# Seven products of quarters in place of a full product in the gated unit of a two-layer trunk

## Chip, core and metric

The kernel runs on one core of a Trainium2 chip. The metric is device time in microseconds (us) of one execution, given as the median of repeated runs. TensorE (PE) multiplies into PSUM; VectorE (DVE), ScalarE (ACT) and GpSimd (POOL) do the elementwise work; all transfers are issued from the queue of SyncE (SP).

## Reference

The reference is a two-layer encoder trunk over 1024 tokens of width 1024, float32. What matters here is the end of the first branch of layer 0 (a state-space layer) and its neighbours:

```
y = gelu(y)                                            # (1024, 1024)
y = y * sigmoid(y @ glu_w + glu_b)                     # the gated unit
y_s5 = y * silu(g_s5)
y_ret = retention(q, k, v) * silu(g_ret)
x = x + concatenate([y_s5, y_ret], -1) @ w_out
```

Layer 1 (a convolution module) and a last RMSNorm follow.

## The kernel before

Activations are kept transposed: channels in 8 blocks of 128 partitions, tokens in two halves of 512 columns. Every large product is made in three matmuls of 128x128 weights by 512 columns (`mm3`, L161 to L168): weights and activations are each split into a high part, rounded on ACT, and a low part, the difference, made on DVE or POOL; high x high, high x low and low x high are added up in one PSUM bank. Products go to three banks (`ps_mm`) in turn.

*Weights* come from one list in program order (`plan`, L75). `wnext` (L105) asks for a weight and issues loads up to two ahead. `wload_pieces` (L146) loads 512 KB into one of three `wf` buffers, rounds it on ACT into one of three `wh` (L157), and makes the low part into one of three `wl` (L158), on POOL except for the names in `LO_V` (L34), which go to DVE. A `wf` buffer is free once both have read it.

*Layer 0* first runs the input projections and the state-space layer (`layer0_front`), which leave y, the gates and the retention's inputs in DRAM. Then `retention` (L860) goes over four pairs of heads: `ret_proj` (L896) projects k and q, multiplies them by the row scale on DVE (L909), swaps halves of the heads by four small DMAs (L918), and turns them on POOL (L922, L924) and DVE (L925). For pair 0 `ret_values_wide` (L961) makes values for two pairs from eight weights, each used for 24 matmuls; pairs 2 and 3 have their own two weights (`ret_values`, L942). Per pair, `y_pass` (L851) takes two blocks of y through the GELU on ACT (L857) into `yn_d` in DRAM. `ret_heads` (L983) does the scores, the state, the norm and the gate, and stores `yr_d`.

*The gated unit* stands at the head of `layer0_back_and_layer1` (L1097). `load_split` (L1107) loads 16 tiles of `yn_d` (8 blocks by 2 halves), two to a `wf` buffer, and splits them (L1092 to L1095) into the operand tiles `opA`. For each of the 8 output blocks, one weight serves two products of 24 matmuls, one for each half (L1135 to L1151): tanh on ACT from PSUM (L1146); gate times y on POOL (L1142) from two loads, `yg` (2 buffers, L1139) and `yn` (3 buffers, L1141); product on DVE (L1147) in one of five `sg` buffers; and the split into `ys` on ACT and DVE (L1149, L1150). Then `yr_d` is loaded and split (L1152), and `w_out` (L1158) multiplies `ys` and `yr` by the output weights.

The order of instructions on each engine is set by a planner that simulates the program with the program's order as priority. `issue_after` forces an instruction behind another one; a DRAM tile that is read waits for its writer. On every engine and in the SP queue the order that results is kept at run time.

Of the kernel before, what the change touches and what calls it, by code (L numbers as in the profile page):

```python
# [19 lines left out]
P = 128  # L20
D = 1024
T = 1024
# [29 lines left out]
class Trunk:  # L52
# [22 lines left out]
    def plan(self):  # L75
# [11 lines left out]
        seq += [(A["w_glu"][nb], f"glu{nb}") for nb in range(8)]  # L87
# [98 lines left out]
    def run(self):  # L186
# [27 lines left out]
        self.yr_d = dt("yr_d", [D, T])  # L214
        self.x1_d = dt("x1_d", [D, T])
# [635 lines left out]
    def y_pass(self, rp, cb):  # L851

        nc = self.nc
        yt = rp.tile([P, 8, P], F32, name=f"yp_{cb}", tag="yp", bufs=1)
        nc.sync.dma_start(yt[:], self.y_d[cb].rearrange("i h g m -> (h g) i m"))
        yn = rp.tile([P, P, 8], F32, name=f"yn_{cb}", tag="ynt", bufs=1)
        nc.scalar.activation(yn[:], yt[:].rearrange("p i m -> p m i"), AF.Gelu_apprx_tanh)  # L857
        nc.sync.dma_start(self.yn_d[cb * P:(cb + 1) * P], yn[:].rearrange("p m i -> p (m i)"))

    def retention(self, st):  # L860
# [13 lines left out]
        for pair in range(4):  # L874
# [21 lines left out]
    def ret_proj(self, pair):  # L896
        nc, A, rp = self.nc, self.A, self.rp
        tq = self.rq.tile([P, 2, T], F32, name=f"ropeq_{pair}", tag="ropeq", bufs=1)
# [3 lines left out]
        def project(nm):  # L902
            w = self.wnext(f"{nm}{pair}")
            raw = raws[nm] = self.rq.tile([P, T], F32, name=f"{nm}raw_{pair}", tag="raw", bufs=2)
            for h in range(2):
# [3 lines left out]
                last = nc.vector.tensor_tensor(raw[:, c], ps[:], self.R[:, c], op=ALU.mult)  # L909
            return last  # L910

        def turn(nm, behind=None):
# [3 lines left out]
            for b in range(4):  # L916
                s = b ^ 1
                nc.sync.dma_start(swp[32 * b:32 * b + 32, :], raw[32 * s:32 * s + 32, :])  # L918
# [4 lines left out]
            for c in cs:  # L923
                nc.gpsimd.tensor_tensor(swp[:, c], swp[:, c], tab[:, 1, c], op=ALU.mult)  # L924
# [15 lines left out]
        yield krot, qrot, qadds  # L940
# [20 lines left out]
    def ret_values_wide(self):  # L961
# [622 lines left out]
```

## Time and profile before

| | |
|---|---|
| median of 3 runs | 1204.49 us (1203.98 to 1204.63) |
| profiled execution | 1205.3 us, of which 1203.5 us from the first to the last instruction |
| mean granted TensorE clock | 0.999 |
| first and last matmul of the gated unit start at | 549.7 and 649.6 us |
| DMA, whole span | 234.19 MB, 195 GB/s mean |

Busy time is the time in which an engine has an instruction in work; for matmuls, which are pipelined, it overlaps. A row of the profile names line, engine, operation, output and inputs, shape, and either one instruction's start and length or a group's count, total and mean. "Idle before" names what ended an engine's wait.

### The profile page before, as it was taken

To read this page: it belongs to the slowest core of one execution; us is meant where nothing else is said; L and a number is where in the kernel's file an instruction comes from. 1 tells how busy PE (TensorE), PEld (TensorE's weight loads), DVE (VectorE), ACT (ScalarE), POOL (GpSimd) and SP (SyncE) were. 2 spreads that over 40 slices of the span, in tenths; PEclk is the share of its full clock that TensorE was granted. 3 is DMA by queue.
4 is the path that set the end of the run, shared out by engine and by line. 5 is a ranking of instruction groups with operands and counts; after the bars stand their busy time and mean duration, and the time that the engine had idled before them with its cause. 6 is when DMAs were issued, how large, how long until landed. Compare 5 with 4: busy or idle time off the path is not lost.

```text
span 1203.5 us, 17285 instructions
## 1 busy us (share of the span) xinstructions
PE 1191.8 (99%) x6442; PEld 999.4 (83%) x6442; DVE 799.5 (66%) x1389; ACT 477.5 (40%) x699; POOL 637.9 (53%) x441
## 2 busy tenths in 40 slices
PE   9999999999999999999999999999999999999997
PEld 7888888888888889998888888888888888888877
DVE  7975798777411457447546322599999799899533
ACT  7212223222223233143435322545535675434652
POOL 2059999988146254242441110678453567758642
PEclk9999999999999999999999999999999999999999
DMA  9344355565385175477448875766678664357774
GB/s 336 105 127 146 102 168 177 184 177 171 108 286 177 53 214 164 148 210 258 157 140 272 302 266 201 245 210 208 211 246 279 204 191 154 114 183 237 238 265 146
DMA packets 105364, 234.19 MB, mean 195 GB/s; under 512 B 9536, under 2 KB 40000, under 8 KB 104640
## 3 DMA queue, kind: packets, MB, share of 16 engines
q1 hardware_dynamic: 105280, 233.09, 58.5%
q8 instruction: 50, 0.82, 0.3%
q14 instruction: 34, 0.28, 0.1%
HBM read 166.80 MB, written 62.06 MB: 190 GB/s over the span
## 4 chain that ended last, share of the span: by engine, by line
PE 95%; DMA 2%; DVE 1%; ACT 1%; issue 0%; POOL 0%; SPq 0%; DVEq 0%; POOLq 0%; ACTq 0%
PE mm_g L166 7%; PE mm_g L167 7%; PE mm_g L168 7%; PE mm_wo L168 5%; PE mm_wo L166 5%; PE mm_wo L167 5%; PE mm_b L167 2%; PE mm_b L168 2%; PE mm_a L167 2%; PE mm_a L168 2%; PE mm_b L166 2%; PE mm_a L166 2%; PE mm_u L168 2%; PE mm_u L167 2%; PE mm_u L166 2%; PE mm_glu L166 2%
## 5 line engine op out<-in xcount | busy, mean ns | idle before, releaser
L1270 DVE SCALAR_TENSOR_TENSOR cv<-u,convw,cv 128x512 f32<-128x512 f32 x398 | 273.4, 751 | 11.9 <-ACT cv L1256 9.6
L1250 POOL TENSOR_TENSOR tp<-tp,tp 128x512 f32<-128x512 f32 x64 | 83.0, 1297 | 44.1 <-ACT tp L1249 43.0
L166 PE MATMUL mm_g<-xh,wh_g 128*128 128x512 f32 x256 | 101.8, 398 | 0.0
L168 PE MATMUL mm_g<-xh,wl_g 128*128 128x512 f32 x256 | 100.1, 391 | 0.0
L167 PE MATMUL mm_g<-xl,wh_g 128*128 128x512 f32 x256 | 100.0, 391 | 0.0
L1249 ACT ACTIVATE tp<-u,convw 128x512 f32<-128x512 f32 x64 | 45.7, 720 | 36.1 <-POOL tp L1250 34.5
L393 POOL TENSOR_TENSOR s1q<-s1q,s1q 128x512 f32<-128x512 f32 x12 | 17.5, 1455 | 78.2 <-ACT s1q L388 78.2
L166 PEld LDWEIGHTS mm_g<-xh,wh_g 128*128 128x128 f32 x256 | 48.0, 188 | 11.7 <-issue 1.2
L168 PEld LDWEIGHTS mm_g<-xh,wl_g 128*128 128x128 f32 x256 | 48.1, 188 | 10.4
L167 PEld LDWEIGHTS mm_g<-xl,wh_g 128*128 128x128 f32 x256 | 48.1, 188 | 9.9 <-issue 0.4
L168 PE MATMUL mm_oc<-zh,wl_woc 128*128 128x512 f32 (+1 forms) x152 | 54.2, 359 | 1.0 <-DMA wl_woc<-lo_woc 1.0
L167 PE MATMUL mm_oc<-zl,wh_woc 128*128 128x512 f32 (+1 forms) x152 | 54.4, 360 | 0.5 <-POOL zl L1095 0.5
L166 PE MATMUL mm_oc<-zh,wh_woc 128*128 128x512 f32 (+1 forms) x152 | 54.1, 361 | 0.0
L1142 POOL TENSOR_TENSOR yg<-yg,yn 128x512 f32<-128x512 f32 x16 | 22.6, 1412 | 57.2 <-DMA yg<-gs_d 28.2
L167 PE MATMUL mm_u<-xl,wh_u 128*128 128x512 f32 x128 | 50.1, 391 | 1.0 <-DVE xl L281 1.0
L349 DVE TENSOR_TENSOR gt<-mm_g,R 128x512 f32<-128x512 f32 x32 | 21.9, 683 | 43.6 <-PE mm_g L168 43.6
L166 PE MATMUL mm_g<-h1h,wh_cg 128*128 128x512 f32 x128 | 50.4, 394 | 0.0
L166 PE MATMUL mm_glu<-yh,wh_glu 128*128 128x512 f32 x128 | 50.3, 393 | 0.0
L166 PE MATMUL mm_b<-h1h,wh_cb 128*128 128x512 f32 x128 | 50.2, 392 | 0.0
L166 PE MATMUL mm_wo<-yrh,wh_wor 128*128 128x512 f32 x128 | 50.2, 392 | 0.0
L168 PE MATMUL mm_a<-h1h,wl_ca 128*128 128x512 f32 x128 | 50.2, 392 | 0.0
L168 PE MATMUL mm_wo<-yrh,wl_wor 128*128 128x512 f32 x128 | 49.9, 390 | 0.0
(417 smaller groups left out, 3613.8 us busy)
## 6 DMA issues: line engine op xcount, KB each, us to landing
wf_g<-w_ab SPq DMA_DIRECT2D x16, 512.0 KB
wf_wos<-w_out SPq DMA_DIRECT2D x16, 512.0 KB
wf_wor<-w_out SPq DMA_DIRECT2D x16, 512.0 KB
wf_cb<-w_c SPq DMA_DIRECT2D x16, 512.0 KB
wf_ca<-w_c SPq DMA_DIRECT2D x16, 512.0 KB
wf_woc<-w_out_c SPq DMA_DIRECT2D x16, 512.0 KB
wf_v<-w_v SPq DMA_DIRECT2D x12, 512.0 KB
wf_cg<-w_c SPq DMA_DIRECT2D x11, 512.0 KB
```

The source lines that it names most:

```text
L166: nc.tensor.matmul(ps, wh[:, kb, :], xh, start=start, stop=False)
L167: nc.tensor.matmul(ps, wh[:, kb, :], xl, start=False, stop=False)
L168: self.last_mm = nc.tensor.matmul(ps, wl[:, kb, :], xh, start=False, stop=stop)
L349: nc.vector.tensor_tensor(gt[:, c], ps[:], self.R[:, c], op=ALU.mult)
L393: nc.gpsimd.tensor_tensor(a, a, sq[:], op=ALU.add)
L1142: gp.tensor_tensor(yg[:], yg[:], yn[:], op=ALU.mult)
L1249: nc.scalar.mul(sk[:], u[:, k:k + HALF], cw[:, nb, k:k + 1])
L1250: gp.tensor_tensor(s0[:], s0[:], sk[:], op=ALU.add)
L1270: v.scalar_tensor_tensor(dst[:], *tap, accs_[i][:], op0=ALU.mult, op1=ALU.add)
```

## The change

The product y @ glu_w is made by Strassen's scheme. With the weights in quarters (by input and output channels) and y in quarters (by channels and token halves), seven products of sums of quarters take the place of eight products of quarters. Each product is four blocks of 12 matmuls.

- `glu_sums`, called four times during retention (after the projections of pairs 0, 2 and 3, and between the two halves of the wide values), loads a quarter of the weights' data in two transfers of 512 KB into two `wf` tiles, makes the four sums in place on DVE behind the pair's last projected q, and stores them to `ws_d` in DRAM behind the last swap.
- `y_pass` takes blocks k and k + 4 in pair k, makes four sums of y in place on POOL behind the last turn, and stores them to `t_d`.
- Masks and decays of retention are loaded per pair instead of once.
- In the gated unit, 28 tiles (seven operands of four) are loaded and split in place of 16, and 14 weights, each used for 24 matmuls, are asked for in place of 8, each used for 48. Four products are copied to `u2` on ACT; sums of products are built in `u2` and `u3` on DVE; the tanh now reads from SBUF a sum that DVE makes from a bank and `u2` or `u3` (`gated`).
- In `w_out` the first block's order is the plain one.

```diff
-        seq += [(A["w_glu"][nb], f"glu{nb}") for nb in range(8)]
+        self.ws_d = self.dram.tile([2, 2, P, 2, KB, P], F32, name="ws_d")
+        quad = lambda i, j, m: A["w_glu"][i, m, :, j]
+        sums = lambda n, m: self.ws_d[n // 2, m, :, n % 2]
+        glu = [q for m in range(2) for q in (quad(0, 0, m), quad(0, 1, m))]
+        glu += [q(m) for q in (lambda m: sums(0, m), lambda m: sums(2, m), lambda m: quad(1, 1, m)) for m in range(2)]
+        glu += [sums(n, m) for m in range(2) for n in (3, 1)]
+        seq += [(q, f"glu{i}") for i, q in enumerate(glu)]
...
-    def y_pass(self, rp, cb):
-
-        nc = self.nc
-        yt = rp.tile([P, 8, P], F32, name=f"yp_{cb}", tag="yp", bufs=1)
-        nc.sync.dma_start(yt[:], self.y_d[cb].rearrange("i h g m -> (h g) i m"))
-        yn = rp.tile([P, P, 8], F32, name=f"yn_{cb}", tag="ynt", bufs=1)
-        nc.scalar.activation(yn[:], yt[:].rearrange("p i m -> p m i"), AF.Gelu_apprx_tanh)
-        nc.sync.dma_start(self.yn_d[cb * P:(cb + 1) * P], yn[:].rearrange("p m i -> p (m i)"))
+    def y_pass(self, rp, k):
+
+
+        nc, gp = self.nc, self.nc.gpsimd
+        yns = []
+        for i, cb in enumerate((k, k + 4)):
+            yt = rp.tile([P, 8, P], F32, name=f"yp_{cb}", tag="yp", bufs=1)
+            nc.sync.dma_start(yt[:], self.y_d[cb].rearrange("i h g m -> (h g) i m"))
+            yn = rp.tile([P, P, 8], F32, name=f"yn_{cb}", tag="ynt", bufs=2)
+            nc.scalar.activation(yn[:], yt[:].rearrange("p i m -> p m i"), AF.Gelu_apprx_tanh)
+            yn = yn[:].rearrange("p m i -> p (m i)")
+            nc.sync.dma_start(self.yn_d[cb * P:(cb + 1) * P], yn)
+            yns.append(yn)
+        (b11, b12), (b21, b22) = ((y[:, :HALF], y[:, HALF:]) for y in yns)
+        with self.tc.issue_after(self.last_turn.ins):
+            gp.tensor_tensor(b22, b22, b12, op=ALU.subtract)
+            gp.tensor_tensor(b12, b12, b11, op=ALU.subtract)
+            gp.tensor_tensor(b11, b22, b11, op=ALU.add)
+            gp.tensor_tensor(b21, b11, b21, op=ALU.subtract)
+        for i in range(2):
+            nc.sync.dma_start(self.t_d[i, k * P:(k + 1) * P], yns[i])
+
+    def glu_sums(self, g):
+
+        nc, v = self.nc, self.nc.vector
+        m, c = g // 2, slice(g % 2 * 4, g % 2 * 4 + 4)
+        q = [self.wp.tile([P, 2, HALF], F32, name=f"wf_gs{i}_{g}", tag="wf", bufs=3) for i in range(2)]
+        for i in range(2):
+            nc.sync.dma_start(q[i][:], self.A["w_glu"][i, m, :, :, c].rearrange("p j k n -> p j (k n)"))
+        (a11, a12), (a21, a22) = ((t[:, 0, :], t[:, 1, :]) for t in q)
+
+        with self.tc.issue_after(self.last_raw.ins):
+            v.tensor_tensor(a22, a21, a22, op=ALU.add)
+            v.tensor_tensor(a21, a11, a21, op=ALU.subtract)
+            v.tensor_tensor(a11, a22, a11, op=ALU.subtract)
+            v.tensor_tensor(a12, a12, a11, op=ALU.subtract)
+        with self.tc.issue_after(self.last_swap.ins):
+            for i in range(2):
+                nc.sync.dma_start(self.ws_d[i, m, :, :, c].rearrange("p j k n -> p j (k n)"), q[i][:])
...
-        self.mask = rp.tile([P, NH, P], F32, name="retmask")
-        nc.sync.dma_start(self.mask[:], A["ret_mask"])
-        self.kdec = rp.tile([P, NH, 64], F32, name="kdec")
-        nc.sync.dma_start(self.kdec[:], A["ret_kdec"])
...
+            if pair != 1:
+                self.glu_sums(pair)
             if pair == 0:
                 V = self.ret_values_wide()
...
-                for cb in (2 * pair, 2 * pair + 1):
-                    self.y_pass(rq, cb)
+                self.y_pass(rq, pair)
...
+        mask = rp.tile([P, 2, P], F32, name=f"retmask_{pair}", tag="retmask", bufs=2)
+        nc.sync.dma_start(mask[:], A["ret_mask"][:, 2 * pair:2 * pair + 2])
+        kdec = rp.tile([P, 2, 64], F32, name=f"kdec_{pair}", tag="kdec", bufs=2)
+        nc.sync.dma_start(kdec[:], A["ret_kdec"][:, 2 * pair:2 * pair + 2])
...
+            if h:
+                self.glu_sums(1)
...
-        def load_split(src, name, halves):
-            res = [[], []]
-
-            def put(kb, h, f):
-                a, b = (self.op_tile(self.opA, f"A{h}", f"{name}{q}{kb}_{h}") for q in "hl")
-                self.split(f, a, b, v, None if halves or h == 0 else self.last_kt if kb < 6 else self.masked[0])
-                res[h].append((a, b))
-            for h in range(2):
-                for kb in range(KB):
-                    if halves:
-                        f = lp.tile([P, HALF], F32, name=f"{name}f{kb}_{h}", tag="tp", bufs=3)[:]
-                        nc.sync.dma_start(f, src[rows(kb), hs(h)])
-                    else:
-
-                        if kb % 2 == 0:
-                            f2 = self.wp.tile([P, 2, HALF], F32, name=f"{name}f{kb}_{h}", tag="wf", bufs=3)
-                        f = f2[:, kb % 2, :]
-                        nc.sync.dma_start(f, src[rows(kb), hs(h)])
-                    put(kb, h, f)
+        def load_split(parts, name, h, wide, behind=None):
+
+            res = []
+            for i, part in enumerate(parts):
+                if wide:
+                    if i % 2 == 0:
+                        f2 = self.wp.tile([P, 2, HALF], F32, name=f"{name}f{i}", tag="wf", bufs=3)
+                    f = f2[:, i % 2, :]
+                else:
+                    f = lp.tile([P, HALF], F32, name=f"{name}f{i}", tag="tp", bufs=3)[:]
+                nc.sync.dma_start(f, part)
+                a, b = (self.op_tile(self.opA, f"A{h}", f"{name}{q}{i}") for q in "hl")
+                self.split(f, a, b, v, behind)
+                res.append((a, b))
...
-        ys_in = load_split(self.yn_d, "y", False)
+
+        B = lambda j, h: [self.yn_d[rows(4 * j + k), hs(h)] for k in range(4)]
+        S = lambda i, h: [self.t_d[i, rows(k), hs(h)] for k in range(4)]
+        b11, b21 = load_split(B(0, 0), "y11", 0, True), load_split(B(1, 0), "y21", 0, True)
         ys = [[None] * KB for _ in range(2)]
-        ws = {}
-
-        for nb, h in [(nb, h) for nb in range(6) for h in range(2)] + [(6, 0), (7, 0), (6, 1), (7, 1)]:
-            if h == 0:
-                ws[nb] = self.wnext(f"glu{nb}")
+
+        u2 = [lp.tile([P, HALF], F32, name=f"gu2_{n}", tag=tag, bufs=1) for n, tag in enumerate(("cq", "cs", "pilot", "sq"))]
+        u3 = [opB.tile([P, HALF], F32, name=f"gu3_{n}", tag="B1") for n in range(4)]
+        nw = iter(range(14))
+        wn = lambda: self.wnext(f"glu{next(nw)}")
+
+        def product(ps, w, a, x):
+            for k in range(4):
+                self.mm3(ps[:], w, 4 * a + k, (x[k][0][:], x[k][1][:]), k == 0, k == 3)
+
+        def gated(nb, h, z):
             yg = lp.tile([P, HALF], F32, name=f"yg{nb}_{h}", tag="ld", bufs=2)
             nc.sync.dma_start(yg[:], self.gs_d[rows(nb), hs(h)])
             yn = lp.tile([P, HALF], F32, name=f"yn{nb}_{h}", tag="ev", bufs=3)
             nc.sync.dma_start(yn[:], self.yn_d[rows(nb), hs(h)])
             gp.tensor_tensor(yg[:], yg[:], yn[:], op=ALU.mult)
-            ps = self.bank(f"mm_glu{nb}_{h}", aux=False)
-            self.gemm(ps[:], ws[nb], ys_in[h])
             sg = lp.tile([P, HALF], F32, name=f"sg{nb}_{h}", tag="u", bufs=5)
-            nc.scalar.activation(sg[:], ps[:], AF.Tanh, scale=0.5, bias=hgb[:, nb:nb + 1])
+            ps, other, op = z
+            v.tensor_tensor(sg[:], other[:], ps[:], op=op)
+            nc.scalar.activation(sg[:], sg[:], AF.Tanh, scale=0.5, bias=hgb[:, nb:nb + 1])
             v.scalar_tensor_tensor(sg[:], sg[:], 1.0, yg[:], op0=ALU.add, op1=ALU.mult)
             a, b = (self.op_tile(opB, f"B{h}", f"ys{q}{nb}_{h}") for q in "hl")
             nc.scalar.mul(a[:], sg[:], 0.5)
-            glu_end = v.scalar_tensor_tensor(b[:], sg[:], 0.5, a[:].bitcast(F32), op0=ALU.mult, op1=ALU.subtract)
             ys[h][nb] = (a, b)
-        yr = load_split(self.yr_d, "yr", True)
+            return v.scalar_tensor_tensor(b[:], sg[:], 0.5, a[:].bitcast(F32), op0=ALU.mult, op1=ALU.subtract)
+
+        for m in range(2):
+            for i, x in ((1, b11), (2, b21)):
+                w = wn()
+                if m == 0 and i == 1:
+                    t2 = load_split(S(0, 0), "yt2", 1, True, self.last_kt)
+                elif i == 1:
+                    t3 = load_split(S(1, 1), "yt3", 1, True, self.masked[0])
+                for a in range(2):
+                    n = 2 * m + a
+                    ps = self.bank(f"mm_glu{i}{n}", aux=False)
+                    product(ps, w, a, x)
+                    if i == 1:
+                        nc.scalar.copy(u2[n][:], ps[:])
+                    else:
+                        gated(n, 0, (ps, u2[n], ALU.add))
+        t4 = load_split(S(1, 0), "yt4", 0, False)
+        for i, x in ((6, t2), (7, t3), (4, t4)):
+            for m in range(2):
+                w = wn()
+                for a in range(2):
+                    n = 2 * m + a
+                    ps = self.bank(f"mm_glu{i}{n}", aux=False)
+                    product(ps, w, a, x)
+                    if i == 4:
+                        gated(4 + n, 0, (ps, u3[n], ALU.subtract))
+                    else:
+                        v.tensor_tensor((u2 if i == 6 else u3)[n][:], u2[n][:], ps[:], op=ALU.add)
+            if i == 6:
+                t1, b22 = load_split(S(0, 1), "yt1", 0, False), load_split(B(1, 1), "y22", 1, False)
+        for m in range(2):
+            for i, x in ((5, t1), (3, b22)):
+                w = wn()
+                for a in range(2):
+                    n = 2 * m + a
+                    ps = self.bank(f"mm_glu{i}{n}", aux=False)
+                    product(ps, w, a, x)
+                    if i == 5:
+                        gated(4 + n, 1, (ps, u3[n], ALU.add))
+                        v.tensor_tensor(u2[n][:], u2[n][:], ps[:], op=ALU.add)
+                    else:
+                        glu_end = gated(n, 1, (ps, u2[n], ALU.add))
+        yr = [load_split([self.yr_d[rows(k), hs(h)] for k in range(KB)], f"yr{h}", h, False) for h in range(2)]
...
-                if nb == 0:
-                    seq.append(seq.pop(KB - 1))
...
-    A["w_glu"] = _blocks(inp["s5_glu_w"][0][s5p][:, s5p])
+
+    wg = inp["s5_glu_w"][0][s5p][:, s5p].reshape(2, 4, P, 2, 2, 2, P)
+    A["w_glu"] = np.ascontiguousarray(wg.transpose(3, 4, 2, 0, 5, 1, 6)).reshape(2, 2, P, 2, KB, P)
```

More of the change, by code (lines that the diff above doesn't have):

```diff
@@ L214, in run @@
         self.yr_d = dt("yr_d", [D, T])
+        self.t_d = dt("t_d", [2, HALF, T])
         self.x1_d = dt("x1_d", [D, T])
@@ L908, in project @@
                 self.gemm(ps[:], w, self.xs[h])
-                last = nc.vector.tensor_tensor(raw[:, c], ps[:], self.R[:, c], op=ALU.mult)
-            return last
+                self.last_raw = nc.vector.tensor_tensor(raw[:, c], ps[:], self.R[:, c], op=ALU.mult)
+            return self.last_raw
         def turn(nm, behind=None):
@@ L939, in ret_proj @@
             qadds = ()
-        yield krot, qrot, qadds
+        yield krot, qrot, qadds, mask, kdec
     def ret_values(self, pair):
@@ L981, in ret_values_wide, with ret_heads @@
         return lambda p, b, hh: res[b // 4][:, b % 4, (2 * p + hh) * P:(2 * p + hh + 1) * P]
-    def ret_heads(self, pair, K, Q, qadds, V, turned):
+    def ret_heads(self, pair, K, Q, qadds, mask, kdec, V, turned):
         nc, rp = self.nc, self.rp
@@ L992, in ret_heads @@
                 nc.tensor.transpose(ps[:, b * P:(b + 1) * P], K[:, t0:t0 + P], self.ident[:])
-            kd = self.kdec[:, 2 * pair:2 * pair + 2, :].rearrange("p h d -> p (h d)")
+            kd = kdec[:].rearrange("p h d -> p (h d)")
             self.last_kt = v.tensor_tensor(kt[:, 4 * hf:4 * hf + 4, :], ps[:].rearrange("p (b d) -> p b d", b=4),
@@ L1035, in ret_heads @@
                     sc[hh][:, 4 * hf:4 * hf + 4, :], sps[hh][:].rearrange("p (b i) -> p b i", b=4),
-                    self.mask[:, 2 * pair + hh, :].unsqueeze(1).broadcast_to([P, 4, P]), op=ALU.mult)
+                    mask[:, hh, :].unsqueeze(1).broadcast_to([P, 4, P]), op=ALU.mult)
         gts = []
```

4 lines of the change are left out of this document (2 added, 2 removed).

## Prediction

> **What bounds the kernel now.** I read the profile page first: span and engine shares, then the chain that ended last.
>
> ```profile
> span 1203.5 us, 17285 instructions
> ...
> PE 1191.8 (99%) x6442; PEld 999.4 (83%) x6442; DVE 799.5 (66%) x1389; ACT 477.5 (40%) x699; POOL 637.9 (53%) x441
> ...
> PE 95%; DMA 2%; DVE 1%; ACT 1%; issue 0%; POOL 0%; SPq 0%; DVEq 0%; POOLq 0%; ACTq 0%
> ```
>
> TensorE (PE) idles 1203.5 - 1191.8 = 11.7 us in the whole span, and the chain of waits is 95% PE. So removed PE work is worth its full length as long as nothing new starves PE, and each new PE stall costs its full length too. Busy time of overlapping matmuls says nothing of their price, so I took the pace from the starts in the timeline of PE, inside the gated unit:
>
> ```profile
> 593.37 0.39 PE L166 MATMUL mm_glu<-yh,wh_glu 128*128 128x512 f32 x1
> 593.60 0.39 PE L167 MATMUL mm_glu<-yl,wh_glu 128*128 128x512 f32 x1
> 593.82 0.39 PE L168 MATMUL mm_glu<-yh,wl_glu 128*128 128x512 f32 x1
> 594.05 0.39 PE L166 MATMUL mm_glu<-yh,wh_glu 128*128 128x512 f32 x1
> ```
>
> Three matmuls in 0.68 us: 0.2267 us each. Next, the busy time of the engines by stage (columns: length, then busy us and count of PE, PEld, DVE, ACT, POOL, then clock, DMA share, GB/s):
>
> ```profile
> 333.00:365.00 32.00, 32.00 (x154) 26.53 (x151) 6.28 (x7) 9.40 (x8) 14.97 (x11) 1.00 0.82 263
> 365.00:400.00 35.00, 35.00 (x159) 28.99 (x158) 4.70 (x3) 11.79 (x16) 18.72 (x8) 1.00 0.52 175
> 581.20:603.00 21.80, 21.80 (x98) 18.00 (x97) 12.46 (x12) 8.11 (x12) 10.46 (x6) 1.00 0.53 181
> ```
>
> The first two rows are retention's first projections and wide values, where the first weight sums are put; the third is the gated unit behind the last heads. Other engines have room, but DMA is at 0.82 in the first. The clock is full, so no price needs scaling. Last, the timelines of ACT, POOL and the DMA queue, for the two places where new work meets old:
>
> ```profile
> 364.11 1.03 ACT L157 CAST wh_v<-wf_v 128x1024 fp32r<-128x1024 f32 x1
> ...
> 360.80 2.85 POOL L158 TENSOR_TENSOR wl_v<-wf_v,wh_v 128x1024 fp32r<-128x1024 f32 x1
> ...
> 365.13 0.98 SPq L155 DMA_DIRECT2D wf_v<-w_v  x1
> ...
> 554.86 6.68 DMA wf_glu<-w_glu
> ...
> 586.24 2.40 POOL L158 TENSOR_TENSOR wl_glu<-wf_glu,wh_glu 128x1024 fp32r<-128x1024 f32 x1
> 586.29 2.90 DVE L1147 SCALAR_TENSOR_TENSOR sg<-sg,yg 128x512 f32<-128x512 f32 x1 [4.17 <-POOL yg L1142]
> ...
> 598.60 0.32 SPq L1139 DMA_DIRECT2D yg<-gs_d  x1
> ```
>
> A weight is loaded only when a subtraction has freed one of three `wf` buffers (360.80 + 2.85 = 363.65, load at 365.13). And a VectorE (DVE) instruction with two SBUF inputs that starts beside a POOL one ends 0.6 us after it (586.29 + 2.90, against 586.24 + 2.40), though it takes 0.68 us alone.
>
> **The change, part by part.**
>
> *Products.* Before: 8 blocks x 2 halves x 8 x 3 = 384 matmuls. After: 7 products x 4 blocks x 4 x 3 = 336. 48 x 0.2267 = **-10.9 us**, all on the chain. The diff leaves no doubt that 336 are issued.
>
> *Weight sums* (`glu_sums`, four calls): each loads 2 x 512 KB into two of the three `wf` buffers, runs 4 additions on DVE behind the last projected `q`, and stores 2 x 512 KB behind the swaps. 16 additions at 0.68 us (alone) to 1.76 (the median of the rotary additions, L925, beside POOL) are 11 to 28 us of DVE, in a stage where DVE is busy 6.28 of 32 and 4.70 of 35 us: covered. What is not covered is the buffers. For pair 0 the calls stand in the program ahead of the third weight of the values, so the buffers freed at about 318 and 333 go to the sums, the third weight (`v002`) gets that of 349 and the fourth (`v003`) that of 363.65, loaded at 365.13 as now a later one is. PE wants `v003` three weights of 24 matmuls after 355.66, at 355.66 + 3 x 5.44 = 372.0. It would be ready at 365.13 + landing + 1.05 (ACT) + 2.40 to 2.85 (POOL). Landing is 3 us (a 256 KB gate load issued at 598.60 is used by POOL at 601.53) to 6.68 us (the chain's row): 371.6 to 375.7, a stall of 0 to 3.7 us. I take **1.5**, as DMA is busy there. The next weights use buffers that the stores give back from about 367 on, 5.44 us apart. The second call, between the value halves, takes the buffers of `v003` and `v010` at about 374 and 377; loads, additions and stores (3 + 3 + 4 us) give them back by about 388, and the last values weight, loaded then, is ready at 388 + 3 + 1.05 + 2.4 = 394.5, wanted at 355.66 + 7 x 5.44 + 1.5 = 395.2: nothing, at most 3 us if the load takes 6.68. The calls of pairs 2 and 3 find weights prefetched over 20 us ahead (`k3` is cast at 469.64 and used from about 494): nothing. If this cover is gone, see the slower rival. The stores wait in SP's queue for DVE; behind them stand the weight loads, which are in the same sum.
>
> *Sums of y*: 16 POOL additions at 1.29 us (L924) = 20.6 us, 5.2 per pair, behind both GELUs of the pair and the last rotary product. POOL is busy 14.97 of 32 and 18.72 of 35 us in the stages above, so they fit; 8 stores of 512 KB stand on SP behind them. The pair's weights, queued behind on POOL, have 5 us of lead: nothing. *Mask and decay by pair*: 8 loads in place of 2, same bytes; six more issues of 0.7 us on SP (L868), used tens of us later: nothing.
>
> *Operands*: 28 splits of y in place of 16: 12 x (0.62 us ACT + 0.69 DVE). 14 weights in place of 8: 6 x (512 KB, 1.05 us ACT, 2.4 to 2.6 us POOL). A weight now lasts PE 5.44 us instead of 10.88; its three `wh` buffers leave 10.9 us for a chain of 1.05 + 2.4 us: 7 us of slack. *Combinations*: 16 additions ahead of the tanh and 12 accumulations on DVE from PSUM at 0.69 us = 19 us, and 4 copies on ACT. A bank must be read within two further products, 5.4 us. *Order of w_out's first block*: `ys` of half 0 is complete after product 4, 22 us earlier: nothing.
>
> *The last twelve products* (4, then 5 and 3 in turn) are all gated: 12 x 2.72 = 32.6 us of PE. POOL: 12 gate products at 1.29 + 4 weights at 2.40 = 25.1 us. DVE with two SBUF inputs: 24 at 0.69 + 2 output weights at 1.22 + 4 splits at 0.69 = 21.7 us. If these two never overlap, 46.8 us must pass in 32.6, so the gated chain ends 14.2 us late. Five `sg` buffers let it lag five products (13.6 us), the banks only two (5.4 us). The stall lies between 0 (lag taken up by `sg`) and 14.2 - 5.4 = 8.8 us. The nearest row, 581.20:603.00, has POOL and DVE at 22.9 us together in 21.80 with PE never idle, so I keep to the lower half: **3 us**. The gate tiles have two buffers: a load is used 2.9 us after issue, then 1.29 + 0.69 us, with waits some 5.5 to 6.5 us per buffer, 2.7 to 3.3 per product against 2.72: within the same lag, not counted again. DMA in these 32.6 us: 24 x 256 KB + 5 x 512 KB + some 2 MB = 11 MB, 330 GB/s; the busiest slice of the page shows 336, so it holds with little over.
>
> [...]
>
> **Sum.** The profiled execution is 1205.3 us, its span 1203.5 and 1.8 around it, 0.8 above the median 1204.49. 1205.3 - 10.9 + 1.5 + 3 = 1198.9; less 0.8: **1198.1**, told as 1198. Bounds: 1204.5 - 10.9 = 1193.6, with all stalls nil, to 1193.6 + 3.7 + 3 + 8.8 = 1209.1.
>
> **Rivals.**
> *All hidden*: no new stall, 1193.6. For it: lags above are bounded by buffers that may suffice; against: DMA at 0.82 where the first sums load.
> *Port-bound tail*: PE waits for banks 8.8 us in the last twelve products; 1193.6 + 8.8 + 1.5 = 1203.9, within the noise. For it: the stretched DVE rows. Against: before, lags of that kind never reached PE.
> *Weights starved in the wide values (slower)*: with two of three `wf` buffers held from load to store, each values weight goes through one buffer: 6.68 + 1.05 + 2.4 = 10.1 us against 5.44 of PE, 4.7 us short each; four such weights are 19 us, 1193.6 + 19 = 1212.6, and with the tail's 3 us 1216. It decides from more than two starved weights (10.9 us). For it: one queue, 0.82 of DMA, stores waiting on DVE. Against: DVE is idle from 365 to 400, so a buffer is held some 12 us, not longer, and two calls, not four, fall in this stage.
>
> **How the numbers follow.** About 0.2% (2.4 us) is what can be told from no change: faster means below 1202.1, slower above 1206.9. Chances: forecast with stalls of 1 to 8 us 0.50; all hidden 0.20; port-bound tail or a like sum 0.10; starved weights 0.20. Faster 0.70, same 0.10, slower 0.20. The range goes from 1193, just under all hidden, to 1210, over the upper bounds and the start of the starved case.
>
> **What would show it.** Right: 336 `mm_glu` matmuls; the value weights' wait near 372 a few us at most; PE's waits inside the last products on banks read by DVE, some us in total; DVE rows of L1147's and L1150's kind with means above 1 us. Wrong: PE idle over 10 us in the wide values (starved); a gap at the first output product, on `wor` or the late splits of `yr`, which I cost at nothing; or PE time in the gated unit not lower by 10.9 us.

## The result, and the profile after

The changed kernel takes 1225.88 us (median of 6 runs, 1221.15 to 1227.66) against 1204.17 us before (1203.59 to 1204.63): ratio 1.0169, 95% interval 1.0156 to 1.0183 (the quotient of the two medians is 1.0180). The forecast was 1198.0, so the result lies 27.9 us above it and 15.9 us above the range. The profiled execution took 1222.3 us, its span 1220.5, so what is explained here are the 17.0 us between the two spans. The median stands 3.6 us higher still: four of the six executions took 1225.2 to 1227.7 us, with a mean granted clock of 0.989 to 0.994 against 0.995 in the profiled one, and what makes them longer is not shown.

Head of the page, and head of the chain, after:

```profile
span 1220.5 us, 17411 instructions
...
PE 1189.3 (97%) x6394; PEld 993.2 (81%) x6394; DVE 849.8 (70%) x1445; ACT 494.6 (41%) x723; POOL 678.9 (56%) x463
...
PE 85%; DVE 6%; DMA 5%; issue 2%; ACT 2%; SPq 0%; POOL 0%; DVEq 0%; ACTq 0%
```

48 matmuls are gone (x6442 to x6394), but idle time of PE rose from 11.7 to 1220.5 - 1189.3 = 31.2 us, and the chain has 15% that is not PE where it had 5%. Where, is told by the windows (columns as before the change):

```profile
365.00:400.00 35.00, 33.66 (x147) 27.06 (x146) 6.23 (x6) 11.05 (x13) 23.62 (x13) 1.00 0.80 273
581.20:603.00 21.80, 17.99 (x79) 14.13 (x78) 19.00 (x44) 11.57 (x17) 7.75 (x4) 0.92 0.40 126
609.00:621.00 12.00, 8.38 (x37) 6.64 (x37) 12.00 (x12) 6.12 (x11) 7.74 (x4) 1.00 0.77 273
```

In the wide values PE idles 1.3 of 35 us. In the gated unit it idles 3.8 of 21.8 us and 3.6 of 12, and there VectorE, which I had at 12.46 of 21.80, is busy 19.00 of 21.80 and then all 12.00. Note 0.92 in the clock's column. The waits of PE (what it waited for, total us, times, longest) name VectorE nearly alone. `S` are the retention's states:

```profile
PE mm_glu L172 <- DVE gu L1224: 4.6, 2, 3.6
PE mm_glu L172 <- DVE sg L1190: 4.0, 3, 2.3
PE sp L1069 <- DVE S L1062: 2.9, 1, 2.9
PE mm_glu L172 <- DVE gu L1236: 2.3, 2, 1.6
PE mm_wo L172 <- DVE gu L1236: 1.8, 1, 1.8
...
PE mm_v L1016 <- ACT wh_v L163: 1.3, 1, 1.3
```

To put a size on each stage I take the starts of PE's groups. The first product starts at 552.22 (before 549.73): 2.5 us lost ahead of it, 2.1 of them in the wide values (45.59 against 43.53). From there to the last of the heads' transposes, PE needs 0.2267 us per product matmul and 13.0 us for the heads (before: 100.1 - 384 x 0.2267); what is above is "lost in heads". This stretch holds the first two products as well: of its waits in the changed kernel (0.9, 2.9, 0.9 and 2.3 us), the last, at 586.43, is a product's wait for a bank. From there to the first output product only matmuls stand; what is above 0.2267 each is "lost in products". After: 10.2 and 14.4 us. So -10.9 + 2.5 + 10.2 + 14.4 + 0.8 (behind the unit) = +17.0.

How a product waits shows in the timeline around the longest wait:

```profile
616.27 2.80 POOL L164 TENSOR_TENSOR wl_glu<-wf_glu,wh_glu 128x1024 fp32r<-128x1024 f32 x1
...
616.78 2.83 DVE L1196 SCALAR_TENSOR_TENSOR ysl<-sg,ysh 128x512 fp32r<-128x512 f32 x1
...
619.54 0.68 DVE L1136 TENSOR_TENSOR y22l<-y22f,y22h 128x512 fp32r<-128x512 f32 x1
620.14 1.27 DVE L1224 TENSOR_TENSOR gu<-gu,mm_glu 128x512 f32<-128x512 f32 x2
...
620.96 0.47 PE L172 MATMUL mm_glu<-yt3h,wh_glu 128*128 128x512 f32 x1 [3.62 <-DVE gu L1224]
...
622.02 0.63 PE L172 MATMUL mm_glu<-yt3h,wh_glu 128*128 128x512 f32 x1
622.44 0.63 PE L173 MATMUL mm_glu<-yt3l,wh_glu 128*128 128x512 f32 x1
```

`ysl` has two SBUF inputs, begins beside a POOL subtraction and ends 0.54 us after it, 2.83 us instead of 0.68. Behind it in order stands a split, and only then the sums (`gu`) that free two banks. PE, with all three banks full, waits 3.62 us. When it resumes, its starts lie 0.43 us apart in place of 0.227, until about 624.6: eight such steps cost 1.6 us more, and the granted clock falls to 0.50.

The heads lose in the same manner:

```profile
560.63 2.53 POOL L164 TENSOR_TENSOR wl_glu<-wf_glu,wh_glu 128x1024 fp32r<-128x1024 f32 x1 [0.86 <-ACT wh_glu L163]
...
561.30 4.22 DVE L1136 TENSOR_TENSOR yt2l<-yt2f,yt2h 128x512 fp32r<-128x512 f32 x4 [0.38 <-ACT yt2h L1134]
...
562.68 0.62 ACT L1134 CAST yt2h<-yt2f 128x512 fp32r<-128x512 f32 x1 [0.26 <-DMA yt2f<-t_d]
563.65 0.62 ACT L1134 CAST yt2h<-yt2f 128x512 fp32r<-128x512 f32 x1 [0.35 <-DMA yt2f<-t_d]
...
565.45 0.28 DVE L1060 COPY S<-kv 128x128 f32<-128x128 f32 x1
...
567.02 1.23 PE L1069 MATMUL sp<-qrot,krot 64*128 64x128 f32 x8 [2.93 <-DVE S L1062]
```

Four splits of `yt2`, an operand first needed 30 us later (at 597.25), stand ahead of the states `S` that the scores wait for. The first of them has two SBUF inputs beside a POOL subtraction, takes 2.42 us and ends 0.56 us after it; the other three follow at 0.60 us each. The casts wait 0.26 and 0.35 us for their loads, but the last is done at 564.27, before its split begins at 564.84.

### The profile page after: what moved, and what is told of

It reads as the page before. It is cut to its first block, busy times and chain, and to the rows that moved or that the text cites. A ratio compares the mean times of both kernels' runs of the same rounds, so it can differ in the third digit from the quotient of the medians.

```text
span 1220.5 us, 17411 instructions
## 1 busy us (share of the span) xinstructions
PE 1189.3 (97%) x6394; PEld 993.2 (81%) x6394; DVE 849.8 (70%) x1445; ACT 494.6 (41%) x723; POOL 678.9 (56%) x463
## 4 chain that ended last, share of the span: by engine, by line
PE 85%; DVE 6%; DMA 5%; issue 2%; ACT 2%; SPq 0%; POOL 0%; DVEq 0%; ACTq 0%
PE mm_g L172 7%; PE mm_g L174 7%; PE mm_g L173 7%; PE mm_wo L172 5%; PE mm_wo L173 5%; PE mm_wo L174 5%; PE mm_b L172 2%; PE mm_b L173 2%; PE mm_a L174 2%; PE mm_b L174 2%; PE mm_a L172 2%; PE mm_a L173 2%; PE mm_u L174 2%; PE mm_u L173 2%; PE mm_u L172 2%; PE mm_oc L174 2%
## 5 line engine op out<-in xcount | busy, mean ns | idle before, releaser
L174 PE MATMUL mm_g<-xh,wl_g 128*128 128x512 f32 x256 | 100.1, 391 | 0.0
L164 POOL TENSOR_TENSOR wl_glu<-wf_glu,wh_glu 128x1024 fp32r<-128x1024 f32 x14 | 36.7, 2622 | 39.3 <-ACT wh_glu L163 36.4
L172 PEld LDWEIGHTS mm_g<-xh,wh_g 128*128 128x128 f32 x256 | 48.0, 188 | 11.7 <-issue 1.2
L172 PE MATMUL mm_wo<-ysh,wh_wos 128*128 128x512 f32 x128 | 50.0, 391 | 1.8 <-DVE gu L1236 1.8
L164 POOL TENSOR_TENSOR wl_v<-wf_v,wh_v 128x1024 fp32r<-128x1024 f32 x12 | 28.9, 2406 | 40.4 <-ACT wh_v L163 40.4
L173 PE MATMUL mm_b<-h1l,wh_cb 128*128 128x512 f32 x128 | 50.3, 393 | 0.0
L172 PE MATMUL mm_a<-h1h,wh_ca 128*128 128x512 f32 x128 | 50.2, 392 | 0.0
```

The costliest lines, as they stand in the source:

```text
L164: lo[i].tensor_tensor(wl[:].rearrange(fl)[:, c], wf[:, c], h.bitcast(F32), op=ALU.subtract)
L172: nc.tensor.matmul(ps, wh[:, kb, :], xh, start=start, stop=False)
L173: nc.tensor.matmul(ps, wh[:, kb, :], xl, start=False, stop=False)
L174: self.last_mm = nc.tensor.matmul(ps, wl[:, kb, :], xh, start=False, stop=stop)
```

## The experiments

Ratios are against the kernel before on the same chip (its median there: 1204.4 to 1205.0 us, and 1204.2 for the change). Most intervals reach 1 to 3 us to either side, so a difference between two of these kernels is good to about 3 us: 10 or 12 us are clear, 1 or 2 us are not. The losses, in us, are from one profiled execution each, worked out as above. That execution lies near the median for most, but 3.6 us below it for the change, 3.1 below for e12, 4.3 above for e2 and 5.9 above for e4.

| kernel | median | ratio, 95% interval | first product | lost in heads | lost in products |
|---|---|---|---|---|---|
| after | 1225.9 | 1.0169 [1.0156, 1.0183] | 552.2 | 10.2 | 14.4 |
| e1 products alone | 1216.3 | 1.0100 [1.0082, 1.0118] | 549.3 | 5.6 | 14.0 |
| e2 preparation alone | 1214.7 | 1.0094 [1.0074, 1.0115] | 556.6 | 6.0 | 0.1 |
| e3 sum in PSUM | 1214.0 | 1.0076 [1.0054, 1.0098] | 553.2 | 11.5 | 2.8 |
| e4 fourth call early | 1227.6 | 1.0201 [1.0168, 1.0234] | 560.4 | | |
| e5 = e1 + e3 | 1204.0 | 0.9995 [0.9985, 1.0004] | 549.3 | 6.4 | 2.6 |
| e11 e3 without sums of y | 1208.8 | 1.0042 [1.0023, 1.0062] | 551.8 | 8.7 | 2.2 |
| e12 e3 without sums of weights | 1207.9 | 1.0029 [1.0017, 1.0041] | 551.1 | 5.9 | 2.6 |
| e13 e5, two operands less | 1197.6 | 0.9938 [0.9923, 0.9953] | 549.5 | -0.5 | 1.6 |
| e14 e3, two operands less | 1203.9 | 0.9995 [0.9983, 1.0006] | 552.8 | 2.3 | 2.0 |
| e16 e3, operands regrouped | 1208.7 | 1.0040 [1.0026, 1.0055] | 553.6 | 4.2 | 5.1 |

**Products or preparation (e1, e2).** e1 takes out the sums; e2 keeps them and puts the gated unit of before back, with its 16 tiles of y, 8 weights and 384 matmuls.

In e1:

```diff
-        sums = lambda n, m: self.ws_d[n // 2, m, :, n % 2]
+        sums = lambda n, m: quad(n // 2, n % 2, m)
...
-            gp.tensor_tensor(b22, b22, b12, op=ALU.subtract)
...
-            if pair != 1:
-                self.glu_sums(pair)
...
-        S = lambda i, h: [self.t_d[i, rows(k), hs(h)] for k in range(4)]
+        S = lambda i, h: [self.yn_d[rows(4 * i + k), hs(h)] for k in range(4)]
```

In e2:

```diff
-        seq += [(q, f"glu{i}") for i, q in enumerate(glu)]
+        seq += [(A["w_glu0"][nb], f"glu{nb}") for nb in range(8)]
...
```

> The sums are left out (no weight sums, no sums of y, none of their loads and stores; the seven products take plain quarters), the gated unit keeps its 336 matmuls, 14 weights, 28 splits and all VectorE work. Theory P (the preparation holds the weight buffers and makes the operands late): the 24 us lost in the gated unit are mostly gone, 1194 to 1200 us. Theory V (VectorE, shared with POOL, is too slow for the unit's own work: bank reads, splits and gating in one queue): the loss stays, 1212 to 1222 us.

> All sums of weights and of y are made and stored as in the changed kernel, but the gated unit is the old one with 384 matmuls, 8 weights, 16 splits, and does not read them. Theory P: most of the loss shows here too, 1212 to 1225 us. Theory V: only what is lost ahead of the unit, 2 to 5 us over the kernel before, 1206 to 1210 us.

The two add up: (1216.3 - 1204.7) + (1214.7 - 1204.7) = 21.6, against 21.7 for the change. Neither theory has it alone: the products bring no gain but cost 11.6 us, and the preparation, which I had at 1.5 us, costs 9.9.

**The second SBUF input (e3, e5).** The sum ahead of the tanh stays in a PSUM bank, so that L1192 and L1196 read one SBUF input instead of two.

```diff
-            sg = lp.tile([P, HALF], F32, name=f"sg{nb}_{h}", tag="u", bufs=5)
...
+            sg = ps_cv.tile([P, HALF], F32, name=f"sg{nb}_{h}", tag=("cv", "cn")[self.nsg % 2])
```

> The sum ahead of the tanh is kept in four PSUM banks that are idle in this stage instead of in SBUF, so that the 32 gating instructions of VectorE read one SBUF operand instead of two; nothing else changes. Theory V with POOL blocking VectorE as its cause: these rows fall to 0.7 us each and 6 to 14 us come back, 1212 to 1220 us. Theory P, or VectorE's own work as the cause: within 3 us of the changed kernel, 1222 to 1228 us.

Groups of VectorE between 585 and 665 us (count, busy us, mean ns, idle before), after and then e3:

```profile
L1196 DVE SCALAR_TENSOR_TENSOR ysl<-sg,ysh 128x512 fp32r<-128x512 f32 x11 | 14.6, 1343 | 0.1
L1192 DVE SCALAR_TENSOR_TENSOR sg<-sg,yg 128x512 f32<-128x512 f32 x12 | 13.6, 1131 | 3.4 <-ACT sg L1191 2.8 <-POOL yg L1187 0.6
L1190 DVE TENSOR_TENSOR sg<-gu,mm_glu 128x512 f32<-128x512 f32 x14 | 9.4, 672 | 2.5 <-PE mm_glu L174 2.5
```

```profile
L1191 DVE TENSOR_TENSOR sg<-gu,mm_glu 128x512 f32<-128x512 f32 x16 | 10.9, 685 | 2.9 <-PE mm_glu L174 2.9
L1193 DVE SCALAR_TENSOR_TENSOR sg<-sg,yg 128x512 f32<-128x512 f32 x14 | 9.7, 692 | 5.7 <-POOL yg L1187 3.2 <-ACT sg L1192 2.4
L1197 DVE SCALAR_TENSOR_TENSOR ysl<-sg,ysh 128x512 fp32r<-128x512 f32 x13 | 8.7, 680 | 0.1
...
L1136 DVE TENSOR_TENSOR y22l<-y22f,y22h 128x512 fp32r<-128x512 f32 x4 | 4.7, 1224 | 1.8 <-ACT y22h L1134 1.8
```

The two forms fall from 1343 and 1131 to 680 and 692 ns, though POOL is as busy as it was (41.5 and 41.3 of the 80 us); the sum itself, with one PSUM input in both, stays at 672 and 685, and the splits, which keep two SBUF inputs, are still stretched in e3 (1224 ns). The loss in products falls from 14.4 to 2.8, the median by 11.9 us, and that with four buffers for the sum in place of five. So in these rows the stretch goes with the second SBUF input. What makes it no run shows; "port" in the prediction and in the expectations is a name for it and no more.

> The seven products with the sum ahead of the tanh kept in PSUM, and no sums made (plain quarters of the weights and of y are loaded in their place, so the numbers it computes are not the unit's). If the loss inside the products is the late reading of banks by VectorE, stretched by GpSimd, it gets back what the same edit got back in the full change (1225.9 to 1214.0, 12 us): 1216.3 - 12 = 1204, with no bank wait behind the heads. If VectorE simply has too much to do, or the time is lost in the heads, the edit gives less than 5 us here: above 1211.

1204.0: the same 12 us without the preparation, as expected. So most of the products' loss goes with the second SBUF input of two rows. What remains is 6.4 us in the heads, 2.6 in the products and 2.2 behind the first output product.

**One call elsewhere (e4).**

```diff
-            if pair != 1:
+            if pair in (0, 2):
                 self.glu_sums(pair)
...
                 self.y_pass(rq, pair)
+            if pair == 2:
+                self.glu_sums(3)
```

> The last of the four calls of weight sums is moved from pair 3, just ahead of the gated unit, to the end of pair 2's projections. Theory P with this call's two weight buffers as the cause: y is loaded some 15 us earlier, the waits from 557 to 590 us go, 1213 to 1219 us. Theory V: 1222 to 1228 us.

No gain (1227.6, its interval overlaps that of the change), although the first tile of y is issued at 530.11 instead of 539.88. The scores now wait for `S` twice, 2.8 us in pair 2 and 5.6 in pair 3.

**What is left in the heads of e3.** The two longest waits are 2.9 us for `S`, as in the timeline above, and 2.8 us for a bank that ScalarE must copy:

```profile
583.95 1.89 DVE L1136 TENSOR_TENSOR yt3l<-yt3f,yt3h 128x512 fp32r<-128x512 f32 x1
...
586.95 0.56 ACT L440 ACTIVATE rs<-mv,epst 128x4 f32<-128x4 f32 x2 [4.10 <-DVE mv L1111]
...
587.42 0.57 ACT L1211 COPY gu<-mm_glu 128x512 f32<-128x512 f32 x1
...
588.04 0.50 PE L172 MATMUL mm_glu<-y11h,wh_glu 128*128 128x512 f32 x1 [2.79 <-ACT gu L1211]
```

A split of `yt3`, 1.89 us beside a POOL subtraction (582.93 to 585.28), stands on VectorE ahead of the heads' statistics `mv`. The root `rs` on ScalarE waits 4.10 us for these, and behind it in order stands the copy that frees the bank.

**Order of the splits (e6, e9).** On e3, the loads of `yt2` and `yt3` go through the small tiles, their splits behind later work on VectorE.

```diff
-                    t2 = load_split(S(0, 0), "yt2", 1, True, self.last_kt)
+                    t2 = load_split(S(0, 0), "yt2", 1, False, self.masked[1])
-                    t3 = load_split(S(1, 1), "yt3", 1, True, self.masked[0])
+                    t3 = load_split(S(1, 1), "yt3", 1, False, self.last_grl)
```

(`last_grl` is the last product at L1127. In e9 the fourth split of `yt2` too stands behind it.)

> The sum in PSUM, and the splits of the third and fourth operand of y (yt2, yt3) loaded through the small tiles in place of the weights' buffers and put behind the last masked scores and the last gated heads on VectorE. Theory (splits that wait for late loads stand in VectorE's queue ahead of the states S and the statistics that the heads wait for): the waits at 568 (3.1 us), 584 (0.8) and 588 (2.8) and the low clock behind them go, 1214.0 - 7 = 1207. Rival (the heads are late because of GpSimd's sums of y and the port): unchanged, 1213 to 1215. If the later splits then come late for their own products, it is above 1214.

> As the run with the later splits, but the fourth split of yt2 too stands behind the last gated head on VectorE (there it waited 6.3 us for its load with the statistics queued behind it). Theory (a split that waits for its load holds up the heads, whatever its place): the 7.7 us wait at the heads' transposes goes and the 3.1 us wait for the states S does not come back; 1217.1 - 8 = 1209, or 1214.0 - 5 = 1209 from the run with the sum in PSUM alone; the splits may then be 1 to 2 us late for the third operand's product. Rival (VectorE's work in the heads, not its order): 1213 to 1216.

Both miss: 1217.1 (ratio 1.0112 [1.0089, 1.0135]) and 1218.8 (1.0119 [1.0090, 1.0148]). The wait for `S` is gone in both, but one of 7.6 and 7.9 us for the heads' statistics has come, so that the heads lose 10.4 and 11.9 us against 11.5 in e3. The rest is lost in the products, 7.6 and 9.2 us against 2.8, where the later splits stand. In e9 VectorE had the statistics ready at 572.4, and the timelines show what was in the way:

```profile
578.03 0.62 ACT L1134 CAST yt2h<-yt2f 128x512 fp32r<-128x512 f32 x1 [9.62 <-DMA yt2f<-t_d]
578.66 1.28 ACT L440 ACT_TABLE_LOAD   x1
579.96 0.49 ACT L440 ACTIVATE rs<-mv,epst 128x4 f32<-128x4 f32 x2
...
584.94 1.30 PE L1124 MATMUL rt<-ident,on 128*128 128x128 f32 x5 [7.93 <-DVE mv L1111]
```

The cast of the fourth tile, left in ScalarE's queue, waited 9.62 us for its load, and the root `rs`, which needs the statistics, stood behind it. A split is a load, a cast and a subtraction on three queues, and I had moved one of them.

**Sums of weights in the front (e7).** The first two calls, in two parts, stand in the last four gate blocks ahead of retention, and no longer in pair 0.

```diff
+            if nb in (20, 22):
+                self.gs_load((nb - 20) // 2)
+            elif nb in (21, 23):
+                self.gs_rest((nb - 21) // 2, True)
```

> The sum in PSUM, and the first two calls of the sums of weights moved out of the projections and wide values of pair 0 into the last four gate blocks ahead of retention. Theory (the held weight buffers starve the wide values): the first product starts 3 us earlier than with the sum in PSUM alone, 1214.0 - 4 = 1210. Rival (VectorE is busy 70% there, and the additions delay the evacuation of the gate blocks as much): 1213 to 1217.

1215.2, ratio 1.0091 [1.0066, 1.0117]: a miss in the total. The wide values are back at 43.52 us, as the theory has it, but the front lost 1.1 us (PE waits 1.6 us for `Kg`) and the heads 1.5 more. On the total alone e7 cannot be told from e3 (1214.0). e6 and e7 together (e8), and e9 and e7 together (e10), were no better than e6 and e9 alone:

> The three edits together. If the three losses are separate, they add: 1214.0 - 7 - 4 = 1203, level with the kernel before; if one cause stands behind two of them, about 1207; if nothing but the bank reads mattered, 1214.

> The same, and the first two calls of the sums of weights in the last gate blocks. That edit alone brought the wide values from 45.8 to 43.5 us, as before the change, but cost 1.1 us in the front, and its total was no better. If its gain was eaten in the heads by waits that the later splits remove: 1 to 2 us below the run beside it, 1207. If not: level with it.

1216.5 (ratio 1.0105 [1.0083, 1.0126]) and 1220.5 (1.0127 [1.0105, 1.0149]): the wait for the statistics, 7.6 and 7.8 us, is in both.

**Which part of the preparation (e11, e12).** Each of the two edits of e1, alone, on e3.

> The sum in PSUM; the sums of y are not made (16 additions on GpSimd and 8 stores left out; quarters of y are loaded in their place). The whole preparation costs 10 us on this base (1214.0 against 1204.0). Theory (the sums of weights hold the buffers, and with them the loads of the weights and of y): 1212 to 1214. Rival (GpSimd's additions and the port delay the heads): 1205 to 1208.

> The sum in PSUM; the sums of weights are not made (16 additions on VectorE, 8 loads and 8 stores of 512 KB left out; quarters of the weights are loaded in their place). Theory (held buffers): 1205 to 1207, with the wide values at 43.5 us, no 3 us wait for S, the first operand of y loaded near 520 to 530. Rival (GpSimd's sums of y): 1211 to 1214.

Neither theory alone: the sums of y cost 5.1 us, those of weights 6.0, which makes 11.1 for the 10 of both. The wide values take 45.76 us in e3, 44.58 without the sums of y, where POOL's additions at 367 to 376 us no longer stand around the weights' lower parts, and 43.52 without those of weights, although the additions for y are still there. In e12 y is loaded from 520.20 on, as the theory has it, and the wait for the bank is gone, but the scores still wait 2.4 us for `S`. In e11 both waits remain (3.2 and 2.5 us), so what the sums of y delay in the heads is not shown.

**Two operands less (e13 on e5, e14 on e3).**

```diff
-                    t2 = load_split(S(0, 0), "yt2", 1, True, self.last_kt)
+                    t2 = b11
-                    t3 = load_split(S(1, 1), "yt3", 1, True, self.masked[0])
+                    t3 = b21
```

> The products alone with the sum in PSUM (no sums made), and products 6 and 7 read the first two operands again, so that the eight loads, casts and splits of the third and fourth operand are left out. Theory (casts and splits that wait for their loads stand ahead of the heads' work in ScalarE's and VectorE's queues): the heads' stage falls from 35.7 to about 30 us and the time from 1204.0 to 1198. Rival (the heads are late for another reason, VectorE's bank reads or the weights' lower parts): 1202 to 1204.

> The full change with the sum in PSUM, and the same eight loads, casts and splits left out. Theory: the heads' stage falls from 40.8 to 30 to 32 us: 1214.0 - 9 = 1205; what is left above the run beside it is the wide values (2 to 3 us) and the values of pair 3 (1 to 2 us). Rival: 1211 to 1214.

1197.6 and 1203.9, 6.4 us below e5 and 10.1 below e3, as the theory has it, and the loss in the heads falls to nothing and to 2.3 us. These kernels take away the work as well as its place.

**Cast and subtraction moved together (e15, e16).** On e3; `yt2` through the small tiles behind the last root `rs`, `yt3` behind `last_grl`.

```diff
-        self.nc.scalar.copy(hi[:], src)
         with self.tc.issue_after(behind.ins) if behind else nullcontext():
+            self.nc.scalar.copy(hi[:], src)
             eng.tensor_tensor(lo[:], src, hi[:].bitcast(F32), op=ALU.subtract)
...
-                    t2 = load_split(S(0, 0), "yt2", 1, True, self.last_kt)
+                    t2 = load_split(S(0, 0), "yt2", 1, False, self.last_rs)
...
```

e16 also takes `yt3` through the small tiles and `yt4` through the weight buffers.

> The full change with the sum in PSUM; cast and split of the third operand (small tiles) stand behind the last root of the heads' statistics on ScalarE, those of the fourth (weight buffers, as in the change) behind the last gated head. Theory: the heads wait no more, 1214.0 - 6 = 1208, unless the two weight buffers held until then starve products 2 or 6: then a wait for a weight of 3 to 8 us takes its place, 1211 to 1216.

> The same with the fourth operand too in small tiles and the fifth in the weight buffers. Theory: no weight is starved, but the loads of the fourth operand begin only when the third is split, so that product 7 may wait 1 to 3 us: 1208 to 1211. If it is at 1214 or above, order cannot be mended in this way.

e15: 1211.5, ratio 1.0058 [1.0038, 1.0078]; e16: 1208.7, the nearest that a kernel with all of the change came to the one before. In e15 no wait for a weight came, and by its interval it cannot be told from e3. Of the 10.1 us, order and the choice of buffers give back 5.3 in e16: the heads lose 4.2 in place of 11.5 us, with a wait of 2.5 us for the normalised heads left, but the products 5.1 in place of 2.8, where the splits now stand.

**The preparation elsewhere (e17, e18).** On e16: first two calls of `glu_sums` in the gate blocks, the others in pairs 1 and 2, and the last quarter of the sums of y in pair 2; in e18 all four calls in the gate blocks.

```diff
-            if pair != 1:
-                self.glu_sums(pair)
+            if pair in (1, 2):
+                self.glu_sums(pair + 1)
...
-                self.y_pass(rq, pair)
+                for k in ((0,), (1,), (2, 3), ())[pair]:
+                    self.y_pass(rq, k)
```

> As the run with the third to fifth operand regrouped (1208.7), with the preparation moved: the first two calls of the sums of weights in the last four gate blocks (the additions behind the evacuation of the block), the other two in pairs 1 and 2, and the last quarter of the sums of y in pair 2, so that pair 3 has none of it. Theory (the preparation costs by where it stands): wide values at 43.5 us, the first operand of y loaded some 10 us earlier, no stretched qrot in the last pair: 1208.7 - 5 = 1204, at best 1201. Rival (it costs by its work, port and buffers, wherever it stands): 1207 to 1211.

> As the run before (1209.9), with all four calls of the sums of weights in the last eight gate blocks, where no heads and no values are. Theory (the sums cost by where they stand): the 3.8 us wait for S in pair 1 and the slow heads behind it go, 1209.9 - 7 = 1203, level with the kernel before. Rival (they cost by their work): 1207 to 1211, with waits in the gate blocks (for the gate weights, or kt for Kg) in place of it.

1209.9 (ratio 1.0042 [1.0025, 1.0059]) and 1210.6 (1.0043 [1.0028, 1.0057]): the rival. The wide values take 44.7 and 45.2 us, although no sums of weights stand there, with PE waiting 0.8 and 1.4 us for a lower part from POOL. Pair 3's scores no longer wait for `S`, but each run has its own new wait of PE, in pair 1 for e17 and in the gate blocks for e18:

```profile
PE sp L1081 <- DVE S L1074: 3.7, 1, 3.7
```

```profile
PE kt L823 <- DVE Kg L821: 2.2, 1, 2.2
```

## Why the prediction was wrong, by its own steps

Two steps were right; in the others a mechanism was missed, and not only a size mis-set. The forecast had stalls of 4.5 us at two places, and the slowest rival, starved weights with 1216 us, neither came nor reached the measured time. The rungs down from 1225.9, each by one run: the second SBUF input 11.9 us (e3), loads, casts and splits of two operands 10.1 (e14), the preparation 6.3 (e14 to e13), down to 1197.6. That this lies next to the 1198.1 of the sum is chance: the sum has the preparation, all operands and 4.5 us of stalls in it, and e13 leaves out the preparation and two operands. The parts also depend on their order: the preparation costs 9.9 us alone (e2), 10.0 on e3 (against e5) and 6.3 on e14.

- *Products, -10.9*: right. In e13, with 336 matmuls and hardly a stall in the unit, the first output product starts 10.1 us earlier than before (639.74 against 649.81). Its median is 7.4 us lower; 2.5 us are lost behind the unit.
- *Wide values, 1.5 (0 to 3.7)*: right in place and size. PE waited 1.33 us for `v003` at 374.25 (forecast 372.0), and the stage is 2.1 us longer. The slower rival of starved weights did not come: one weight was late, not four.
- *The last twelve products, 3 (0 to 8.8)*: right there: by the starts PE stood 1.7 + 0.9 + 1.9 us from the first of them to the first output product. The sum left out VectorE's own 16 bank reads there, though: 16 x 0.69 = 11.0 us, which with the 21.7 fill the 32.6 us even without any stretch. And the step failed in where it begins: I let the lag of VectorE begin with the last twelve products and held the eight ahead of them (6 and 7) for covered. There PE stood 0.8 + 1.2 + 1.2 + 3.8 us, and lost 1.6 by the low clock behind the last; with the 4.5 above that is 13.1 of the 14.4 us. The wait of 2.3 us at 586.43, in the first product, is of the same kind. The 5.4 us in which a bank must be read is no slack when VectorE reads it in order behind a stretched `ysl` and a split.
- *Operands and combinations, no cost*: with the second SBUF input the step that failed most, 10.1 us for eight of the loads, casts and splits. I listed 12 more splits by their work on two engines with idle time (the "7 us of slack" was worked out for the weights alone) and did not ask what is queued behind each on its engine. Idle time of an engine was no cover, since a split that is stretched beside POOL (2.42 us at 561.30, 1.89 at 583.95) and a cast that waits for its load (9.62 us in e9) keep their place.
- *Sums of y, "nothing"*: 5.1 us. I compared busy POOL with its idle time, and the pair's weights with a lead of 5 us; 1.2 us of it shows in the wide values, and only beside the sums of weights; where the rest arises is not shown. The stretched `qrot` of pair 3 (2.63 us for two, 1.64 before) is not their doing: it stands beside `wl_glu` (557.40 to 559.77) and took 3.10 us in e11.
- *Calls in pairs 2 and 3, "nothing"*: with the first two 6.0 us. I looked at the weights' prefetch, not at what else passes through `wf`: the first tile of y was issued at 539.88, 19.6 us later than before, behind the stores of the fourth call. That this late load is what costs is not shown: in e4 and e17 it was issued at 530.11 and 525.63, without a gain.
- *The stretch beside POOL, 3 out of 0 to 8.8*: that VectorE's rows with two SBUF inputs and POOL's never overlap was my assumption, and no run shows it; the runs show rows that begin beside a POOL subtraction and end 0.54 us (616.78) and 0.56 us (561.30) after it. For the last twelve products the 4.5 us measured lie nearer to the 3. But I priced the stretch in these twelve alone, and with one SBUF input in two forms of instruction the kernel gained 11.9 us (e3): this step was mis-sized by its reach. I kept to the lower half since no lag had ever reached PE before; but before, ScalarE read the banks, and VectorE's lag could not.

What stays open: the 6.3 us of the preparation could not be moved away in any of the places that I tried, so whether a better one exists is not known; and e13 and e14 do not part the place of the two operands from their work, beyond the 5.3 us that order and buffers gave back in e16.

## What to carry to other kernels

A saving of matmuls was worth its length here only where the engine that now frees the banks had room in order, not on average (the first output product 10.1 us earlier in e13, 14.4 us lost in the products of the change): for each instruction added to a queue, write down what stands behind it and what it waits for, on every one of the queues that the step touches. An operand that is needed 30 us later should not be cast or split ahead of work that is needed at once, though moving it gave back only half of its price here. Where rows of VectorE with two SBUF inputs are seen stretched beside GpSimd, try one of the inputs in PSUM if it comes from there: here the rows fell from 1343 and 1131 to 680 and 692 ns, and that one line was worth 12 us.

## What was not expected of the hardware

In these traces some stalls of PE cost more than the wait. After the 3.62 us wait at 620.96 the granted clock was 0.62, 0.50 and 0.74 in the next three stretches of 1.5 us and matmuls started 0.43 us apart, 1.6 us lost on top. The 2.9 us wait at 567.02 and the 2.3 us wait at 586.43 were followed by 0.50 for some 3 us as well, the waits of 0.7 to 1.8 us by none. A wait of 2.51 us at 581.11 in e18 was followed by starts 0.43 us apart, one of the same 2.51 us at 584.44 in e17 by starts 0.23 us apart, so the length of the wait does not decide it alone; what does is not shown.
